# Layer 0's adaLN weight tiles in one list, eleven of them used in the first stage: a two-layer trunk on one Trainium2 core

## The chip, the cores and the metric

The kernel runs on one core of a Trainium2 chip. The metric is the device time of one execution, in microseconds. The engines are called by the names of the profile: PE (TensorE, matrix products; PEld is its weight load), DVE (VectorE), ACT (ScalarE), POOL (GpSimd) and SP (SyncE, which here only issues DMAs, one after the other).

## What is computed

A decoder trunk of two layers on 256 tokens of width 2048, in float32. Layer 0 has a Conformer convolution as its mixer, layer 1 has differential attention, and each layer ends with an MLP of width 8192. Every sub-layer is modulated by six vectors (shift, scale and gate of the mixer, shift, scale and gate of the MLP), which come from one matrix per layer: `cond @ ada_w[i]`, 2048 by 12288, 100 MB in float32 for each layer, read for a single row.

```python
cond = silu(c)
for i in range(2):
    sh_m, sc_m, g_m, sh_f, sc_f, g_f = split(cond @ ada_w[i] + ada_b[i], 6)
    h = x * (1 + sc_m) + sh_m
    y = conformer_conv(h, ...) if i == 0 else diff_attention(h, ...)
    x = layer_norm(ALPHA * x + g_m * y, ...)
    h = x * (1 + sc_f) + sh_f
    y = square(relu(h @ mlp_w1[i] + b1)) @ mlp_w2[i] + b2
    x = layer_norm(ALPHA * x + g_f * y, ...)

def conformer_conv(h, ...):
    a, gt = split(h @ pw1 + b1, 2)              # 2048 -> 4096
    u = a * sigmoid(gt)
    u = causal_depthwise_conv(u, width=31)
    return silu(layer_norm(u, ...)) @ pw2 + b2   # 2048 -> 2048
```

The large products are made to float32 accuracy from three passes: weights and activations are each split in a high part (fp32r, a copy on ACT) and a low part (the rest, a subtraction on DVE), and PE adds up high by high, high by low and low by high.

## The kernel before

**Stages of layer 0, mixer.** pw1 runs in five slices of the contraction dimension (`SLICES`, line 32: 2, 2, 4, 4 and 4 blocks of 128). A slice has 8 output groups of 512 columns and works in *halves*: a half is two blocks by two token tiles by three passes, 12 matmuls. There are 8 halves in each of the first two slices and 16 in each of the others. The slice's partial sums are added up on DVE (`add_up`, line 939). While a slice runs, the adaLN scale and shift for the blocks of the next one are made, in pairs of tiles (`ada_pair`, at the halves in `PAIR_AT`), then finished (`end_ada`, at `END_AT`), and the next slice's h is written (`put_h`, one call for two blocks). The last slice also runs the first convolution steps by a plan (`run_plan`). Behind pw1 comes the *conv tail*, 12 steps (lines 1053 to 1056), then the channel LayerNorm with the *fills* (lines 1065 to 1106), the gate, `swish`, and the product pw2 with its residual (`out_proj`, 16 weight tiles; behind each, `pump_t2` is called once). The MLP of layer 0 follows, then layer 1.

**adaLN tiles.** An adaLN tile is 1024 KB. There are two ways to use one. A *D tile* covers 1024 columns and 2 of the 16 row blocks; DVE multiplies each block by its column of `cond` and adds it up (line 248, two instructions), and after eight tiles PE sums over the partitions (line 231) and DVE adds the bias. A *P tile* covers 512 columns and 4 row blocks; PE multiplies it (line 289), and after four tiles the row is copied by ACT and transposed by PE (line 272). The pairs of the first stage (scale on DVE, shift on PE) are 32 narrower tiles. The 48 *later* tiles are the gate of the mixer and the scale and shift of the MLP: 32 D and 16 P. The gate has to be there before the fills end (line 1086), the others when the MLP begins.

**Two mechanisms.** The pairs are loaded from a list of their own, `ada_load`, five ahead, two more after each pair. The later tiles have a second list, `ada_seq`, of which four are loaded ahead: `ada_ahead` loads one, and `ada_next` uses one and loads another. The first four are loaded in the last slice, at halves 2, 8, 9 and 10; none is used before the conv tail. The tail uses 12 (8 D and 4 P, in the order `ADA_CONV`), the fills use 6 P, and the 16 calls of `pump_t2` spread the other 30 (24 D and 6 P).

**Buffers.** `ada_raw` (line 194) gives each load its home. In the mode "first" five homes take turns: two buffers of their own ("own"), two parts of `ux`, and part of `conv_x`. In the mode "conv" an own buffer alternates with a weight buffer. In the mode "pw2" it is own, part of `ux`, own, part of `conv_x`. `ux` and `conv_x` are the buffers of the convolution and are occupied by it from the middle of the last slice to the end of the tail. A load waits on SP until the tile that had its home before has been used, and later requests on SP stand behind it. pw1's weights are loaded four tiles (eight halves) ahead and split two halves ahead (`split_half`, line 888); a split is a cast on ACT (L481) and a subtraction on DVE (L482).

**Order.** In this first part DVE, ACT and SP run in the order of the program text (`manual_schedule`, line 868), and so does PE throughout. Behind it ACT, SP and POOL are ordered by the framework's planner, DVE again by hand from pw2 on.

Of the kernel before, what the change touches and what calls it, by code (L numbers as in the profile page):

```python
# [19 lines left out]
P = 128  # L20
D = 2048
# [10 lines left out]
SLICES = ((0, 2), (2, 2), (4, 4), (8, 4), (12, 4))  # L32
PAIR_AT = ((1, 3), (0, 2, 3, 5), (1, 4, 7, 10), (1, 4, 7, 10), ())
END_AT = (5, 6, 12, 12, None)
STAGE = ((9, 11), (13, 15), (16, 17), (18, 19), (20, 21), (22, 23), (24, 25), (26, 27))
ADA_CONV = "DPDDPDDPDDPD"
FILL = (1, 1, 2, 2)
ADA_MLP = 66
ADA_WO = 8
ADA_T2 = 16  # L40
# [38 lines left out]
def trunk(  # L79
# [111 lines left out]
    def mod_tile(i, v):  # L191
        return const.tile([P, KC], F32, name=f"mod_{i}_{v}")

    def ada_raw(name):

        homes = {"first": ("own", "own", ux[:, :2048], ux[:, 2048:], conv_x[:, :2048]),
                 "conv": ("own", "weights"), "pw2": ("own", ux[:, 2048:], "own", conv_x[:, :2048])}[n_raw[1]]
        home = homes[n_raw[0] % len(homes)]
        n_raw[0] += 1
        if not isinstance(home, str):  # L200
            return home
        pool, tag = (wraw, "raw") if home == "weights" else (araw, "araw")
        return pool.tile([P, 2048], F32, tag=tag, name=name)

    n_raw = [0, "first"]
    ux = big.tile([P, 4096], F32, tag="uTh", name="conv_ux")
    conv_x = econv.tile([P, 8 * (PAD + S + 1)], F32, name="conv_x")
# [131 lines left out]
                defer(SUM_WAIT, sums)  # L339
        return [lambda kc=kc: step(kc) for kc in range(KC)]  # L340

    ada_q, ahead, later_ada = [], [], {"D": [], "P": []}
# [20 lines left out]
    assert not any(later_ada.values()) and len(ada_seq) == 48  # L363
# [506 lines left out]
    ada_load, ada_step, ada_end = [], [], []  # L870
    for f0, nf in SLICES:
        sc = ada_slice_dve_steps(0, SC_M, f0, nf, m_sc)
        sh = ada_slice_steps(0, SH_M, f0, nf, m_sh, True)
        for a in range(len(sc[0])):
            ada_load.extend([sc[0][a], sh[0][a]])
        ada_step.append([(sc[1][a], sh[1][a]) for a in range(len(sc[0]))])
        ada_end.append((sc[2], sh[2]))
    w_src = [(f"pw1_{g}_{s}", pw1v[:, f0:f0 + nf, :, g * 256:(g + 4 // nf) * 256])
             for s, (f0, nf) in enumerate(SLICES) for g in range(0, NGRP, 4 // nf)]
# [20 lines left out]
    def pending():  # L900
        fns = later[:]
        later.clear()
        for f in fns:
            f()

    def ada_pair(s):
        rows, sh_step = ada_step[s].pop(0)
        n = len(rows) // 2
        for f in rows[:n]:
            f()  # L910
        sh_step()

        def rest():
            for f in rows[n:]:
                f()
            for _ in range(2):
                if ada_load:
                    ada_load.pop(0)()
        later.append(rest)

    def alpha_x(q):

        sl = slice(q * NG, (q + 1) * NG)
        for t in range(NT):
            nc.scalar.activation(z[:, t, sl], z[:, t, sl], AF.Copy, scale=ALPHA)

    def end_ada(s):
        for f in ada_end[s]:
            f()

    def put_h(s, c2):
        f0, nf = SLICES[s]
        if 2 * c2 == f0:
            nc.vector.tensor_scalar(mul[:, f0:f0 + nf], m_sc[:, f0:f0 + nf], 1.0, None, ALU.add)
        to_featT(z, hT, mul, m_sh, "h0", [c2])()
        if c2 % 2:
            later.append(lambda: alpha_x(c2 // 2))
# [5 lines left out]
            else:  # L943
                nc.vector.tensor_tensor(cs[g]["ut"][t], cs[g]["ut"][t], pss[t], op=ALU.add)

    for _ in range(4):
        ada_load.pop(0)()
# [4 lines left out]
    ada_load.pop(0)()  # L952
# [12 lines left out]

# [19 lines left out]

    for j, c in enumerate(STAGE):
        for e in range(2):
            at(c[e] + 1, conv_out, j, e)
    for j, c in enumerate(STAGE):
        for e in range(2):  # L990
            at(c[e] + 2, conv_tok, j, e)
    for j, c in enumerate(STAGE):
        at((4, 6)[j] if j < 2 else STAGE[j - 2][0], glu, j)
    at(23, lambda: nc.scalar.activation(warm, ones[:, 0:1], AF.Silu))
    for j, c in enumerate(STAGE):
        for e in range(2):
            at(c[e], conv_products, j, e)
    for j, c in enumerate(STAGE):
        for b in range(4):
# [14 lines left out]
    for s, (f0, nf) in enumerate(SLICES):  # L1014
        last = f0 + nf == KC
        h = 0
        for g in range(NGRP):
            pss = [mm_bank(f"pw1_{g}_{s}_ps{t}") for t in range(NT)]
            for q in range(nf // 2):
                split_half()  # L1020
                mm_parts(pss, hT, w_parts.pop(0), f0 + 2 * q, f0, f0 + nf - 1)
                pending()
                if h in PAIR_AT[s]:
                    ada_pair(s + 1)
                if not last and h >= END_AT[s]:
# [32 lines left out]
    n_raw[:] = [0, "pw2"]  # L1058

    def fill(n):  # L1060
        for _ in range(n):
# [88 lines left out]
    n_t2 = [0]  # L1150

    def pump_t2():
        n_t2[0] += 1
        if n_t2[0] == 1:
            n_t2.append(len(ahead) + len(ada_seq))
        while len(ahead) + len(ada_seq) > max(0, n_t2[1] * (1 - n_t2[0] / ADA_T2)):
            ada_next()
        if n_t2[0] == GF_LOAD:
            gf_load[0]()
            gf_load[1]()  # L1160
# [313 lines left out]
    for g in range(4):  # L1474
        kv = {}
        pair = lambda: sc1["hT"]
# [85 lines left out]
```

## Time and profile before

| | |
|---|---|
| three runs of before | 2408.17, 2415.34 and 2418.0 us; median 2415.34 |
| the profiled execution | 2417.05 us, of which the span from the first to the last instruction is 2414.5 us |
| mean granted clock of PE | 0.978 |
| busy, share of the span | PE 95%, PEld 75%, DVE 75%, ACT 44%, POOL 10% |
| read from HBM | 604.54 MB; 251 GB/s over the span |

Rows of the profile name an instruction by engine, line, operation, and out<-in by the names of the tiles. In a row of the timeline, the first two numbers are the start and the duration in microseconds, and a bracket at the end gives the idle time of the engine before it and what ended it. In the view by windows each row is a stretch, with its length, the busy time of each engine, PE's granted clock as a share of full speed, the busy share of the 16 DMA engines and the GB/s. In the view of waits, the numbers are microseconds in total, times, and the longest. In a row of the groups, `x` is the count, and after the bar stand busy microseconds, mean nanoseconds of one, and the idle time before. Tiles that are called `aw`, `conv_ux` or `conv_x` and are loaded on line 218 are adaLN tiles; `aacc` is a D tile's sum, `aps` a P tile's.

### The profile page before, as it was taken

Reading aid. Unit: us, or ns where it says so; the run is one execution under the profiler, and the core shown is the slowest. Engines: PE = TensorE matmul, PEld = TensorE weight load, DVE = VectorE, ACT = ScalarE, POOL = GpSimd, SP = SyncE. Lnnn points to the kernel's source line nnn. Section 1 sums busy time; section 2 is a strip of 40 time slices with the busy share of each in tenths; the row PEclk is TensorE's granted clock in tenths of the full one; section 3 lists DMA queues with packets and bytes.
Section 4 is the critical chain, followed back from the end, with each engine's and each line's share of the span. In section 5 each row is a group of like instructions: output and inputs, shape, how many; then the busy total and the mean of one; then the engine's idle time right before and its main releaser. Section 6 shows DMA issues by size and latency. Waiting matters only on the chain.

```text
span 2414.5 us, 28618 instructions
## 1 busy us (share of the span) xinstructions
PE 2287.4 (95%) x11167; PEld 1820.8 (75%) x11167; DVE 1803.1 (75%) x2046; ACT 1057.5 (44%) x1360; POOL 247.9 (10%) x162
## 2 busy tenths in 40 slices
PE   5899988889999999999989999998999999999997
PEld 4577645667778888888877888876788888888886
DVE  5787878879797888877877777886877565565566
ACT  4334753244334434434434445444443443443442
POOL 0000001121330000000024201012213000000002
PEclk9999998989999999999999999998999999999999
DMA  9995389958898888888865666684777555556563
GB/s 347 327 326 199 109 300 367 364 177 321 314 317 313 294 317 289 315 299 307 305 226 181 220 218 227 228 312 164 253 266 225 191 191 192 192 187 194 180 223 104
DMA packets 271980, 608.54 MB, mean 252 GB/s; under 512 B 11038, under 2 KB 44388, under 8 KB 258532
## 3 DMA queue, kind: packets, MB, share of 16 engines
q1 hardware_dynamic: 271604, 606.41, 72.5%
q8 instruction: 87, 1.43, 0.2%
q14 instruction: 49, 0.40, 0.0%
q10 hardware_dynamic: 240, 0.30, 0.0%
HBM read 604.54 MB, written 2.13 MB: 251 GB/s over the span
## 4 chain that ended last, share of the span: by engine, by line
PE 77%; DVE 11%; DMA 5%; issue 3%; ACT 3%; SPq 1%; POOL 1%; DVEq 0%; ACTq 0%; POOLq 0%
PE w_ps L568 18%; PE w_ps L571 18%; PE w_ps L570 18%; DVE aacc L248 2%; DMA aw<-in_ada_w_dram 2%; PE pw_ps L493 2%; PE pw_ps L494 2%; PE pw_ps L495 2%; PE cv L771 2%; DVE wl_w L533 1%; PE qkv_q_ps L571 1%; PE aps L289 1%; PE qkv_q_ps L570 1%; PE qkv_q_ps L568 1%; PE qkv_v_ps L571 1%
## 5 line engine op out<-in xcount | busy, mean ns | idle before, releaser
L533 DVE TENSOR_TENSOR wl_w<-w_w,wh_w 128x1024 fp32r<-128x1024 f32 x502 | 634.4, 1281 | 333.0 <-ACT wh_w L532 332.6
L532 ACT CAST wh_w<-w_w 128x1024 fp32r<-128x1024 f32 x512 | 537.4, 1053 | 763.7 <-PE w_ps L571 589.1
L568 PE MATMUL w_ps<-wh_w,hm_hi 128*128 128x512 f32 x1024 | 403.9, 394 | 4.8 <-ACT hm_hi L401 4.8
L570 PE MATMUL w_ps<-wl_w,hm_hi 128*128 128x512 f32 x1024 | 400.8, 391 | 4.9 <-DVE wl_w L533 4.8
L570 PE MATMUL w_ps<-wl_w,u_hi 128*128 128x512 f32 x1024 | 399.6, 390 | 4.8 <-DVE wl_w L533 4.8
L571 PE MATMUL w_ps<-wh_w,hm_lo 128*128 128x512 f32 x1024 | 401.0, 392 | 0.9 <-DVE hm_lo L404 0.9
L568 PE MATMUL w_ps<-wh_w,u_hi 128*128 128x512 f32 x1024 | 400.5, 391 | 0.0
L571 PE MATMUL w_ps<-wh_w,u_lo 128*128 128x512 f32 x1024 | 399.3, 390 | 0.0
L315 DVE SCALAR_TENSOR_TENSOR acc<-adaw,cond,acc 128x2048 f32<-128x2048 f32 (+1 forms) x105 | 243.1, 2315 | 1.1 <-DMA adaw<-in_ada_w_dram 0.9
L568 PEld LDWEIGHTS w_ps<-wh_w,hm_hi 128*128 128x128 f32 x1024 | 193.5, 189 | 49.1 <-ACT hm_hi L401 6.5
L570 PEld LDWEIGHTS w_ps<-wl_w,hm_hi 128*128 128x128 f32 x1024 | 193.4, 189 | 45.4 <-DVE wl_w L533 6.1
L570 PEld LDWEIGHTS w_ps<-wl_w,u_hi 128*128 128x128 f32 x1024 | 192.5, 188 | 46.2 <-DVE wl_w L533 6.7
L571 PEld LDWEIGHTS w_ps<-wh_w,hm_lo 128*128 128x128 f32 x1024 | 193.3, 189 | 43.1 <-DVE hm_lo L404 2.5
L568 PEld LDWEIGHTS w_ps<-wh_w,u_hi 128*128 128x128 f32 x1024 | 192.6, 188 | 42.4 <-issue 1.7
L571 PEld LDWEIGHTS w_ps<-wh_w,u_lo 128*128 128x128 f32 x1024 | 192.5, 188 | 39.9
L533 POOL TENSOR_TENSOR wl_w<-w_w,wh_w 128x1024 fp32r<-128x1024 f32 x10 | 24.1, 2421 | 1096.7 <-ACT wh_w L532 1096.7
L493 PE MATMUL pw_ps<-wh_pw,h_hi 128*128 128x512 f32 x256 | 106.1, 414 | 12.1 <-ACT h_hi L401 9.3
L482 DVE TENSOR_TENSOR wl_pw<-w_pw,wh_pw 128x1024 fp32r<-128x1024 f32 x64 | 77.7, 1221 | 33.6 <-ACT wh_pw L481 33.3
L494 PE MATMUL pw_ps<-wl_pw,h_hi 128*128 128x512 f32 x256 | 101.8, 398 | 0.5 <-DVE wl_pw L482 0.5
L495 PE MATMUL pw_ps<-wh_pw,h_lo 128*128 128x512 f32 x256 | 101.9, 398 | 0.0
L481 ACT CAST wh_pw<-w_pw 128x1024 fp32r<-128x1024 f32 x64 | 65.9, 1050 | 48.0 <-PE pw_ps L495 40.6
L248 DVE SCALAR_TENSOR_TENSOR aacc<-aw,cond,aacc 128x1024 f32<-128x1024 f32 (+2 forms) x70 | 75.8, 1083 | 2.8 <-DMA aw<-in_ada_w_dram 1.1
(335 smaller groups left out, 3274.7 us busy)
## 6 DMA issues: line engine op xcount, KB each, us to landing
w_w<-in_mlp_w_dram SPq DMA_DIRECT2D x256, 1024.0 KB, 5.2
adaw<-in_ada_w_dram SPq DMA_DIRECT2D x96, 1024.0 KB, 5.2
aw<-in_ada_w_dram SPq DMA_DIRECT2D x48, 1024.0 KB, 10.8
w_pw<-in_conv_pw_w_dram SPq DMA_DIRECT2D x64, 512.0 KB, 9.1
conv_ux<-in_ada_w_dram SPq DMA_DIRECT2D x21, 1024.0 KB, 11.6
w_pw<-in_conv_pw_w_dram SPq DMA_DIRECT2D x16, 1024.0 KB, 10.5
w_qkv_q<-in_attn_qkv_w_dram SPq DMA_DIRECT2D x16, 1024.0 KB, 7.2
w_qkv_k<-in_attn_qkv_w_dram SPq DMA_DIRECT2D x16, 1024.0 KB, 5.0
```

The lines of the kernel that those rows point to most:

```text
L248: nc.vector.scalar_tensor_tensor(st["acc"], wv[:, kc % per, :], cond[:, kc:kc + 1], st["acc"], ALU.mult, ALU.add)
L315: nc.vector.scalar_tensor_tensor(st["acc"], w, cond[:, kc:kc + 1], st["acc"], ALU.mult, ALU.add)
L481: nc.scalar.copy(hq, rq)
L482: nc.vector.tensor_tensor(lq, rq, hq.bitcast(F32), op=ALU.subtract)
L493: nc.tensor.matmul(pss[t], lhsT=xh, rhs=wh, start=(kc == first), stop=False)
L494: nc.tensor.matmul(pss[t], lhsT=xh, rhs=wl, start=False, stop=False)
L495: nc.tensor.matmul(pss[t], lhsT=xl, rhs=wh, start=False, stop=(kc == last))
L532: nc.scalar.copy(hi, rq)
L533: eng.tensor_tensor(lo, rq, hi.bitcast(F32), op=ALU.subtract)
L568: nc.tensor.matmul(pss[tt], lhsT=xh, rhs=wh, start=(kc == 0 and job["bias"] is None), stop=False)
L570: nc.tensor.matmul(pss[tt], lhsT=xh, rhs=wl, start=False, stop=False)
L571: nc.tensor.matmul(pss[tt], lhsT=xl, rhs=wh, start=False, stop=(kc == nk - 1))
```

## The change

All of layer 0's adaLN tiles go into one list, `items`, in the order of use: the pairs of each slice, the new extra tiles between them, the tail's, and those of fills and pw2. Each entry has its mode, its load and its use. `load_ahead` loads while fewer than `limit` are loaded and not used; `used(n)` counts uses and loads on. The limit is 4 at the start, then 5, 2 from half 11 of the fourth slice on, and 4 from half 9 of the last slice on.

Eleven of the later tiles are used in pw1 (`EXTRA`): one D after half 14 of the third slice (blocks 4 to 7), two D after halves 13 and 15 of the fourth, and eight in the last slice: P after halves 0, 4, 8, 10 and 14, D after 2, 6 and 12. The first three have homes of the mode "first"; the eight use a new mode "own", the two own buffers alone. The tail then takes the next 8 D and 4 P, the fills 6 P, and 18 D and 1 P are left for pw2. The mode "pw2" begins with the first fill tile instead of the fifth. Each half of the last slice now ends with a tick, which runs finishes that are due.

At the very start, `end_ada(0)` and `put_h(0, 0)` stand ahead of the first two `split_half()`.

```diff
+EXTRA = ({}, {}, {14: "D"}, {13: "D", 15: "D"},
+         {0: "P", 2: "D", 4: "P", 6: "D", 8: "P", 10: "P", 12: "D", 14: "P"})
-AHEAD_ADA = 4
...
         homes = {"first": ("own", "own", ux[:, :2048], ux[:, 2048:], conv_x[:, :2048]),
-                 "conv": ("own", "weights"), ...
+                 "own": ("own",), "conv": ("own", "weights"), ...
...
-    ada_seq = []
-    for e in ADA_CONV + "P" * sum(FILL) + "DDDDP" * 8:
-        if later_ada[e]:
-            ada_seq.append(later_ada[e].pop(0))
-
-    def ada_ahead():
-        if ada_seq:
-            load, step = ada_seq.pop(0)
-            load()
-            ahead.append(step)
+    def add_items(mode, kinds):
+        for e in kinds:
+            if later_ada[e]:
+                items.append((mode, *later_ada[e].pop(0)))
+
+    def load_ahead():
+        while n_items[1] < len(items) and n_items[1] - n_items[0] < limit[0]:
+            mode, load, _ = items[n_items[1]]
+            if n_raw[1] != mode:
+                n_raw[:] = [0, mode]
+            load()
+            n_items[1] += 1
+
+    def used(n):
+        n_items[0] += n
+        load_ahead()
 
     def ada_next(n=1):
         for _ in range(n):
-            if ahead:
-                ahead.pop(0)()
-                ada_ahead()
+            if n_items[0] < n_items[1]:
+                items[n_items[0]][2]()
+                used(1)
...
+        pair = [[("first", sc[0][a], None), ("first", sh[0][a], None)] for a in range(len(sc[0]))]
+        for h in range(-1, 16):
+            if s == 0 and h < 0:
+                items.extend(i for p in pair for i in p)
+            elif s and h in PAIR_AT[s - 1]:
+                items.extend(pair.pop(0))
+            if s and h in EXTRA[s - 1]:
+                add_items("first", EXTRA[s - 1][h])
+    extra = [EXTRA[-1][h] for h in sorted(EXTRA[-1])]
+    add_items("own", extra)
+    add_items("conv", ADA_CONV)
+    add_items("pw2", "P" * sum(FILL) + "DDDDP" * 8)
...
         def rest():
             for f in rows[n:]:
                 f()
-            for _ in range(2):
-                if ada_load:
-                    ada_load.pop(0)()
+            used(2)
...
+    end_ada(0)
+    put_h(0, 0)
     for _ in range(2):
         split_half()
-    end_ada(0)
-    put_h(0, 0)
...
                 if last:
                     run_plan(h)
-                    if h in (2, 8, 9, 10):
-                        if h == 2:
-                            n_raw[:] = [0, "conv"]
-                        ada_ahead()
+                    tick()
+                    if h == 9:
+                        limit[0] = 4
+                if h in EXTRA[s]:
+                    ada_next()
+                if s == len(SLICES) - 2 and h == 11:
+                    limit[0] = 2
```

More of the change, by code (lines that the diff above doesn't have):

```diff
@@ L194, in ada_raw @@
     def ada_raw(name):
-        homes = {"first": ("own", "own", ux[:, :2048], ux[:, 2048:], conv_x[:, :2048]),
+        homes = {"first": ("own", "own", ux[:, :2048], ux[:, 2048:], conv_x[:, :2048]), "own": ("own",),
                  "conv": ("own", "weights"), "pw2": ("own", ux[:, 2048:], "own", conv_x[:, :2048])}[n_raw[1]]
@@ L340, in ada_steps @@
         return [lambda kc=kc: step(kc) for kc in range(KC)]
-    ada_q, ahead, later_ada = [], [], {"D": [], "P": []}
+    ada_q, items, n_items, limit = [], [], [0, 0], [5]
+    later_ada = {"D": [], "P": []}
     def add_later(eng, v, f0, m):
@@ L358, in trunk @@
     add_later("P", SH_F, 8, m_shf)
-    ada_seq = []
-    for e in ADA_CONV + "P" * sum(FILL) + "DDDDP" * 8:
-        if later_ada[e]:
-            ada_seq.append(later_ada[e].pop(0))
-    assert not any(later_ada.values()) and len(ada_seq) == 48
-    def ada_ahead():
-        if ada_seq:
-            load, step = ada_seq.pop(0)
+    def add_items(mode, kinds):
[7 more added lines that the diff above has]
+                n_raw[:] = [0, mode]
             load()
-            ahead.append(step)
+            n_items[1] += 1
+    def used(n):
+        n_items[0] += n
+        load_ahead()
     def ada_next(n=1):
         for _ in range(n):
-            if ahead:
-                ahead.pop(0)()
-                ada_ahead()
+            if n_items[0] < n_items[1]:
+                items[n_items[0]][2]()
+                used(1)
     m_gf = mod_tile(0, G_F)
@@ L869, in trunk @@
     first_part.__enter__()
-    ada_load, ada_step, ada_end = [], [], []
-    for f0, nf in SLICES:
+    ada_step, ada_end = [], []
+    for s, (f0, nf) in enumerate(SLICES):
         sc = ada_slice_dve_steps(0, SC_M, f0, nf, m_sc)
         sh = ada_slice_steps(0, SH_M, f0, nf, m_sh, True)
-        for a in range(len(sc[0])):
-            ada_load.extend([sc[0][a], sh[0][a]])
         ada_step.append([(sc[1][a], sh[1][a]) for a in range(len(sc[0]))])
         ada_end.append((sc[2], sh[2]))
+        pair = [[("first", sc[0][a], None), ("first", sh[0][a], None)] for a in range(len(sc[0]))]
[10 more added lines that the diff above has]
+    add_items("pw2", "P" * sum(FILL) + "DDDDP" * 8)
+    assert not any(later_ada.values())
     w_src = [(f"pw1_{g}_{s}", pw1v[:, f0:f0 + nf, :, g * 256:(g + 4 // nf) * 256])
@@ L944, in add_up @@
                 nc.vector.tensor_tensor(cs[g]["ut"][t], cs[g]["ut"][t], pss[t], op=ALU.add)
-    for _ in range(4):
-        ada_load.pop(0)()
+    limit[0] = 4
+    load_ahead()
     for t in range(NT):
@@ L951, in trunk @@
         load_w()
-    ada_load.pop(0)()
+    limit[0] = 5
+    load_ahead()
     load_small(0, "conv", [conv_pw1_b[0], conv_dw_b[0], conv_ln_g[0], conv_ln_b[0]])
@@ L1033, in trunk @@
                     run_plan(h)
-                    if h in (2, 8, 9, 10):
-                        if h == 2:
-                            n_raw[:] = [0, "conv"]
-                        ada_ahead()
+                    tick()
+                    if h == 9:
+                        limit[0] = 4
+                if h in EXTRA[s]:
+                    ada_next()
+                if s == len(SLICES) - 2 and h == 11:
+                    limit[0] = 2
                 h += 1
@@ L1057, in trunk @@
     first_part.__exit__(None, None, None)
-    n_raw[:] = [0, "pw2"]
     def fill(n):
@@ L1154, in pump_t2 @@
         if n_t2[0] == 1:
-            n_t2.append(len(ahead) + len(ada_seq))
-        while len(ahead) + len(ada_seq) > max(0, n_t2[1] * (1 - n_t2[0] / ADA_T2)):
+            n_t2.append(len(items) - n_items[0])
+        while len(items) - n_items[0] > max(0, n_t2[1] * (1 - n_t2[0] / ADA_T2)):
             ada_next()
```

## The prediction, on record before the change was run

> **What bounds the kernel now.** I read the page's 40 slices first, to find where the DMA is full and where PE is, and then cut the span into the stages of the code with the view of busy time by windows.
>
> ```profile
> core 0: us, PE busy (x) PEld busy (x) DVE busy (x) ACT busy (x) POOL busy (x), PEclk, DMA share, GB/s
> 32.50:100.00 67.50, 58.71 (x273) 41.69 (x274) 48.42 (x72) 27.11 (x38) 0.00 (x0) 0.93 1.07 372
> ...
> 156.00:207.40 51.40, 51.09 (x246) 38.37 (x246) 42.02 (x56) 20.19 (x24) 0.00 (x0) 1.00 0.71 233
> 207.40:270.80 63.40, 61.26 (x427) 47.17 (x425) 49.01 (x87) 39.18 (x57) 0.00 (x0) 1.00 0.39 134
> 270.80:334.80 64.00, 61.41 (x926) 33.56 (x925) 56.48 (x111) 51.42 (x93) 0.00 (x0) 0.97 0.53 191
> 334.80:355.70 20.90, 12.41 (x85) 5.07 (x84) 9.50 (x23) 12.07 (x20) 0.72 (x1) 0.85 1.04 392
> 355.70:502.30 146.60, 124.06 (x528) 90.48 (x525) 119.58 (x110) 41.61 (x50) 22.69 (x9) 0.88 0.96 358
> 502.30:2414.50 1912.20, 1856.19 (x8388) 1519.85 (x8386) 1421.21 (x1498) 836.14 (x1038) 222.54 (x142) 0.99 0.70 241
> ```
>
> The rows are: early pw1, its fourth slice, its last slice, the conv tail, the fills, pw2, and all the rest. Three readings carry the argument. Up to 100 us the DMA is full (1.07). From 156 to 271 PE is full (51.09 of 51.40 us, 61.26 of 63.40) and the DMA has room (0.71, then 0.39). In the fills and pw2 the DMA is full again (1.04, 0.96), and PE has a low granted clock (0.85, 0.88). After 502 PE is busy 97% of the time with work that the change leaves alone, so a microsecond won or lost before 502 should be one at the end. PE's own waits in pw2, complete:
>
> ```profile
> PE aps L289 <- DMA aw<-in_ada_w_dram: 10.0, 2, 6.0
> PE aps L289 <- DMA conv_x<-in_ada_w_dram: 5.1, 2, 4.8
> PE apt L231 <- DVE aacc L248: 4.6, 2, 3.6
> PE aps L289 <- DMA conv_ux<-in_ada_w_dram: 2.9, 1, 2.9
> ```
>
> 18.0 of 22.6 us are P tiles (the adaLN tiles that PE multiplies, line 289) that stand in PE's queue before their data has landed. None is a wait for pw2's own weights.
>
> **What leaves pw2.** Of the 48 later tiles pw2 takes 30 now (24 for DVE, called D, and 6 P) and 19 afterwards (18 D, 1 P). The tail (8 D, 4 P) and the fills (6 P) keep their counts. One tile is one megabyte:
>
> ```profile
> aw<-in_ada_w_dram SPq DMA_DIRECT2D x48, 1024.0 KB, 10.8
> ```
>
> Eleven are 11.5 MB. At pw2's 358 GB/s that is 32.2 us of DMA, at the 392 of the fills 29.4. PE's side allows as much: five of six P tiles go, and with them up to 18.0 us of waits, 5 x 1.1 us of matmuls (row below) and part of the 146.6 x 0.12 = 17.6 us lost to the clock. DVE's side:
>
> ```profile
> L248 DVE SCALAR_TENSOR_TENSOR aacc<-aw,cond,aacc 128x1024 f32<-128x1024 f32 x21 | 35.1, 1671 | 1.7 <-DMA aw<-in_ada_w_dram 1.1
> ...
> L248 DVE SCALAR_TENSOR_TENSOR aacc<-conv_x,cond,aacc 128x1024 f32<-128x1024 f32 x12 | 17.5, 1458 | 0.3
> L248 DVE SCALAR_TENSOR_TENSOR aacc<-conv_ux,cond,aacc 128x1024 f32<-128x1024 f32 x12 | 17.4, 1451 | 0.3
> ```
>
> These 45 instructions take 70.0 us, 1.56 each; a D tile is two, 3.1 us. The same instruction in the conv tail:
>
> ```profile
> L248 DVE SCALAR_TENSOR_TENSOR aacc<-aw,cond,aacc 128x1024 f32<-128x1024 f32 x15 | 19.2, 1280 | 0.3
> ```
>
> 1.28 us, 2.56 a tile, and POOL is idle there (0.00) where it is busy 22.69 us in pw2. Six D tiles are thus 15.4 to 18.7 us off DVE's 119.6. [...] Nothing in the sum hangs on it: DVE's remaining 101 to 104 us lie under the new length either way.
>
> So the DMA sets the gain. I take -28 us for fills and pw2: a little under 29.4, since at a share of 0.96 not every removed transfer was waited for. Bounds: -15 (only DVE's relief counts) and -38 (the DMA's 32, and some of the clock). What is late next in pw2 is DVE and PE together. For its 384 matmuls PE needs 88 us at the spacing of 0.23 us that full clock gives (rows below), and DVE the 101 to 104 above, both against 146.6 - 28 = 119.
>
> The last four of the six fill tiles change homes: two now wait on SP, in program order, for the conv's last use of its buffers.
>
> ```profile
> L528 SPq DMA_DIRECT2D w_pw<-in_conv_pw_w_dram x3: 464/2202/2415, 331.2 to 339.5; - x3
> ```
>
> ```profile
> L218 SPq DMA_DIRECT2D conv_x<-in_ada_w_dram x1: 2576/2576/2576, 335.2 to 335.2; - x1
> ```
>
> The first request for pw2's weights, at 331.2, may then queue behind a request for conv_x, which before went out at 335.2: at most +4. It also frees two weight buffers that fill tiles held, which may bring it forward by as much. I take 0.
>
> **What the first stage takes on.** P tiles, seen in the fourth slice:
>
> ```profile
> 161.66 0.39 PE L494 MATMUL pw_ps<-wl_pw,h_hi 128*128 128x512 f32 x1
> 161.90 0.39 PE L495 MATMUL pw_ps<-wh_pw,h_lo 128*128 128x512 f32 x1
> 162.21 1.07 PE L289 MATMUL aps<-aw,condr 128*32 128x512 f32 x8
> 163.21 0.50 PE L493 MATMUL pw_ps<-wh_pw,h_hi 128*128 128x512 f32 x1
> ```
>
> From start to start a matmul is 0.23-0.24 us; across the P tile it is 1.31, so the tile costs 1.1. Five in the PE-bound last slice are +5.5, with nothing to hide them; their finishing transposes add 0.5. Six.
>
> D tiles run on DVE in program order, so the weight subtractions (L482) behind them wait 2.56 us. Three lie where DVE is at its latest, at the slice changes, behind the second half's h:
>
> ```profile
> 157.24 0.69 DVE L404 TENSOR_TENSOR h_lo<-h_h,h_hi 128x512 fp32r<-128x512 f32 x1 [1.29 <-ACT h_hi L401]
> 158.19 1.22 DVE L482 TENSOR_TENSOR wl_pw<-w_pw,wh_pw 128x1024 fp32r<-128x1024 f32 x1 [0.26 <-ACT wh_pw L481]
> ```
>
> ```profile
> 159.47 0.50 PE L494 MATMUL pw_ps<-wl_pw,h_hi 128*128 128x512 f32 x1 [0.31 <-DVE wl_pw L482]
> ```
>
> PE already waits 0.31 for this one. The D tile of half 14 falls between the two DVE rows: the subtraction starts 2.56 later less the 0.26 of idle, and PE stops 2.3 us more. At the next change two D tiles come, after halves 13 and 15 (the last rows of this DVE view; its first is used further down):
>
> ```profile
> 195.67 1.22 DVE L482 TENSOR_TENSOR wl_pw<-w_pw,wh_pw 128x1024 fp32r<-128x1024 f32 x1
> ...
> 208.58 0.69 DVE L404 TENSOR_TENSOR h_lo<-h_h,h_hi 128x512 fp32r<-128x512 f32 x1 [1.29 <-ACT h_hi L401]
> 209.53 1.23 DVE L482 TENSOR_TENSOR wl_pw<-w_pw,wh_pw 128x1024 fp32r<-128x1024 f32 x1 [0.26 <-ACT wh_pw L481]
> 210.67 1.28 DVE L944 TENSOR_TENSOR sums<-sums,pw_ps 128x512 f32<-128x512 f32 x2
> 211.87 1.22 DVE L482 TENSOR_TENSOR wl_pw<-w_pw,wh_pw 128x1024 fp32r<-128x1024 f32 x1
> ```
>
> The first moves 209.53 to about 211.9, the second 211.87 to about 217. A half on PE is 12 x 0.23 = 2.8 us, so PE reaches these at about 211.6 (after a P tile) and 215.7 and stops about 1.5 and 2.3 us: +3.8. The three in the last slice meet a DVE that is idle 63.4 - 49.0 = 14.4 us; 7.7 us go into that, but DVE is sometimes late there, so +2. Together +8; bounds 0 (all hidden) and 15.4 (six tiles in full). First stage: 6 + 8 = +14, from +6 to +22.
>
> The SP queue: from the third extra of the last slice on, each tile goes into one of only two buffers, so SP asks for it when the tile two before it has been used, and weight requests stand behind. Landing there, adaLN tiles first, then weights:
>
> ```profile
> DMA to landing us min/median/max: 5.0/6.2/7.4
> ```
>
> ```profile
> DMA to landing us min/median/max: 3.9/4.6/5.2
> ```
>
> Two tiles are four halves apart, 11 us and more. 6.2 fits under that: 0. The tail's first four tiles are asked for at halves 10 to 14 instead of 2 to 10; with 6.2 us to land they are there when the tail begins at 270.8: 0. The tick that each half of the last slice now ends with runs only what the extra tiles have put off (their finishes, counted above). POOL's queue is passed by nothing: it has no work before the fills (0.00 in the rows).
>
> First h ahead of the first casts: the first matmul waited for h_hi behind two casts, and then for DMA.
>
> ```profile
> 32.54 0.79 PE L493 MATMUL pw_ps<-wh_pw,h_hi 128*128 128x512 f32 x1 [7.64 <-ACT h_hi L401]
> ...
> 41.10 1.07 PE L289 MATMUL aps<-aw,condr 128*32 128x256 f32 x16 [1.40 <-DMA aw<-in_ada_w_dram]
> ```
>
> ```profile
> 26.73 1.99 ACT L481 CAST wh_pw<-w_pw 128x1024 fp32r<-128x1024 f32 x2 [5.40 <-DMA w_pw<-in_conv_pw_w_dram]
> ```
>
> The first of these two casts (half of 1.99) and its subtraction (1.22 in the rows above), one after the other from 26.73, let PE begin near 29, 3.5 us sooner. But at 41.10 it waits for a tile of a full DMA, and 1.40 becomes 4.9. I take 0; if that cover is gone, -3.5.
>
> Sum: -28 + 14 = -14. The profiled execution took 2417.05 us, so 2403; the median of before is 1.7 lower, so 2401.
>
> **Rivals.** *More comes back* (0.20). P tiles no longer stop PE in pw2, its clock stays up, and the D tiles hide: -36 + 8 = -28, so 2415.3 - 28 = 2387. For it: the P waits and the clock of 0.88. Against it: the L494 wait at 159.47.
>
> *DVE takes over pw2* (0.15). DVE is busy 119.58 of 146.6 us, in one order, with casts between tiles. If that order paces pw2, only the 15.4 us of six tiles come off, against +14: 2415.3 - 1.4 = 2414, no change. Against: PE's waits for DVE there are only 4.6.
>
> *SP holds the weights back* (0.10), the way to slower. The third tile for the two buffers is asked for when the last pair of adaLN tiles has been used, just before the DVE row at 195.67, and SP then stands until the last slice's first P tile has run: 207.4 + 2.8 + 1.1, near 211. The next weights behind are wanted ten halves after 196, 27.6 us; 12 are left. Tile ahead (2.7 us of transfer), landing, cast and subtraction (2.3) must fit, so it decides from a landing of 7 us. At 11, PE stops 4 us here and at each of five later requests: +24 on the +14, less 28, is +10: 2425. Against: 4.6 and 6.2. [...]
>
> **How the numbers follow.** Forecast 0.55, its own range 2391 to 2412 (half the spread of each term). A measurement of this kernel can tell 0.5%, 12 us: below 2403.3 is faster. Forecast gives 0.33 faster and 0.22 the same; with the first rival, faster 0.53; with the second, the same 0.37; slower 0.10. The range, 2384 to 2419, takes in the first rival to a little past its middle and the second with some of its spread; outside lie the third (0.10) and the far end of the first.
>
> **What would show it.** Right: the first matmul near 29 and the next wait for a tile at 41 unmoved; pw1 ends some 14 us later than 270.8, with L494 waits at both slice changes; the tail is as long as before (64.0); fills and pw2 are 28 us shorter than 20.9 + 146.6, with hardly a P wait and a clock above 0.88. Wrong: PE waiting for ACT casts that wait for w_pw in the last slice (third rival); pw2 still 130 us or more with DVE over 95% busy (second); the first stage no longer at all (first).

## The result, and the profile after

| | before | after |
|---|---|---|
| median of the runs, us | 2416.33 (2408.17 to 2418.0, 4 runs) | 2393.42 (2391.37 to 2394.6, 4 runs) |
| the profiled execution, and its span, us | 2417.05, 2414.5 | 2392.5, 2390.7 |
| mean granted clock of PE | 0.978 | 0.987 |

The ratio is 0.9911, with a 95% interval from 0.9887 to 0.9935: 23 us by the medians, where 14 were forecast, and inside the range. The view by windows of the kernel after, cut at the same places as that of before in the prediction (early pw1, its last slice, the tail, the fills, pw2, and everything from the MLP's first product on), with the last stretch of before behind it:

```profile
32.50:100.00 67.50, 56.64 (x280) 40.00 (x278) 46.37 (x72) 25.26 (x36) 0.00 (x0) 0.95 1.05 368
...
209.00:283.30 74.30, 69.47 (x472) 49.28 (x472) 58.89 (x98) 39.93 (x58) 0.00 (x0) 1.00 0.57 192
283.30:353.30 70.00, 65.17 (x944) 36.31 (x943) 59.28 (x117) 55.48 (x97) 0.00 (x0) 0.98 0.60 218
353.30:372.60 19.30, 10.31 (x69) 4.10 (x68) 7.22 (x18) 8.60 (x17) 0.72 (x1) 0.82 1.05 393
372.60:484.30 111.70, 105.97 (x484) 82.57 (x480) 106.83 (x96) 39.93 (x47) 22.98 (x9) 0.98 0.97 358
...
491.00:2390.70 1899.70, 1848.03 (x8355) 1515.08 (x8355) 1413.08 (x1484) 833.38 (x1029) 217.09 (x140) 0.99 0.71 242
```

```profile
514.20:2414.50 1900.30, 1850.78 (x8359) 1517.31 (x8355) 1409.51 (x1481) 830.91 (x1028) 214.77 (x137) 0.99 0.70 242
```

The last slice and the tail are longer, fills and pw2 much shorter (131.0 us for 167.5), and in pw2 PE now runs at 0.98 of its clock where it ran at 0.88. The DMA is as full there as before (0.97, 358 GB/s). PE's own waits in the fills, and then in pw2, complete:

```profile
PE aps L290 <- DMA conv_x<-in_ada_w_dram: 7.0, 1, 7.0
PE aps L290 <- DMA conv_ux<-in_ada_w_dram: 1.6, 1, 1.6
PE aps L290 <- DMA aw<-in_ada_w_dram: 0.4, 1, 0.4
```

```profile
PE pw_ps L580 <- DVE wl_pw L543: 5.6, 2, 4.4
```

In pw2 there is no P wait left, and the one kind of wait is for DVE.

For the stages below I use four landmarks of each trace: the last pw1 matmul, the end of the last convolution matmul (the tail's end), the end of the last pw2 matmul, and the first matmul of the MLP. Before they are at 270.4, 334.1, 502.5 and 514.2, after at 282.7, 353.0, 484.3 and 490.9. So pw1 gives 12.4 us away and the tail 6.6; fills and pw2 win 37.1; the change from pw2 to the MLP wins 5.1 (11.7 to 6.7); the rest wins 0.5. That makes the 23.8 between the two spans.

Differences of 2 to 3 us near 110 us, behind the stretch where the DMA is full (1.06 from 100 to 104 us, before), are taken as no evidence: in the trace of before and in the four below whose program is the same up to there, one and the same subtraction of DVE lies between 106.4 and 108.6 us.

### The profile page after: what moved, and what is told of

It reads as the page before. It is cut to its first block, busy times and chain, and to the rows that moved or that the text cites. A ratio compares the mean times of both kernels' runs of the same rounds, so it can differ in the third digit from the quotient of the medians.

```text
span 2390.7 us, 28609 instructions
## 1 busy us (share of the span) xinstructions
PE 2276.4 (95%) x11167; PEld 1814.2 (76%) x11167; DVE 1802.4 (75%) x2046; ACT 1059.9 (44%) x1360; POOL 247.6 (10%) x162
## 4 chain that ended last, share of the span: by engine, by line
PE 78%; DVE 12%; DMA 4%; issue 3%; ACT 2%; POOL 1%; SPq 1%; DVEq 0%; ACTq 0%; POOLq 0%
PE w_ps L578 18%; PE w_ps L581 18%; PE w_ps L580 18%; DVE aacc L249 2%; PE cv L781 2%; PE pw_ps L503 2%; PE pw_ps L504 2%; PE pw_ps L505 2%; DVE wl_w L543 1%; DVE acc L316 1%; PE qkv_q_ps L581 1%; PE qkv_q_ps L580 1%; PE qkv_q_ps L578 1%; PE qkv_v_ps L581 1%; PE qkv_v_ps L578 1%
## 5 line engine op out<-in xcount | busy, mean ns | idle before, releaser
L503 PEld LDWEIGHTS pw_ps<-wh_pw,h_hi 128*128 128x128 f32 x256 | 49.3, 192 | 40.1 <-issue 15.6
```

The lines of the kernel that those rows point to most:

```text
L503: nc.tensor.matmul(pss[t], lhsT=xh, rhs=wh, start=(kc == first), stop=False)
```

## The experiments

Medians of each kernel, each against the kernel before on the same chip, and the landmarks of its trace (fills and pw2: from the tail's end to the last pw2 matmul):

| kernel | median, us | ratio to before, 95% interval | tail's end | fills and pw2 |
|---|---|---|---|---|
| before | | | 334.1 | 168.4 |
| after | 2393.42 | 0.9911 [0.9887, 0.9935] | 353.0 | 131.3 |
| before, eleven loads shared | 2407.92 | 0.9976 [0.9965, 0.9987] | 333.1 | 158.3 |
| before, eleven uses cut | 2405.33 | 0.9969 [0.9959, 0.9979] | 334.2 | 154.7 |
| before, both | 2391.53 | 0.9910 [0.9896, 0.9925] | 333.0 | 145.7 |
| before, both, finishes later | 2386.48 | 0.9889 [0.9876, 0.9903] | 332.0 | 138.9 |
| after, homes of before | 2398.05 | 0.9941 [0.9922, 0.9959] | 352.8 | 134.3 |
| after, casts first | 2395.65 | 0.9930 [0.9909, 0.9950] | 352.6 | 131.6 |
| after, P tiles only | 2400.75 | 0.9941 [0.9921, 0.9960] | 336.0 | 149.2 |
| after, D tiles only | 2415.04 | 1.0008 [0.9997, 1.0020] | 357.4 | 145.1 |
| after, D tiles in mid-slice | 2394.97 | 0.9925 [0.9912, 0.9939] | 348.6 | 133.5 |
| after, early pw2 weights | 2404.16 | 0.9965 [0.9952, 0.9977] | 360.9 | 133.3 |
| after, eight tiles | 2400.89 | 0.9944 [0.9930, 0.9958] | 341.2 | 147.4 |

There is one trace of each kernel, so a difference of 2 or 3 us between two stages rests on single executions: the work from the MLP's first product to the end, the same in all, takes 1898.7 to 1902.8 us in these traces. The four runs of "P tiles only" span 2393.9 to 2402.8 us, and its trace is that of the lowest. The trace of "before, both" is that of its highest run (2395.32 us; the other three lie between 2390.6 and 2391.7).

**The bytes alone.** The kernel before, with eleven loads left out and the tile ahead used twice.

```diff
         def load(a):
+            if share[0]:
+                return share[1].rearrange("p (j n) -> p j n", n=w)
-            t = ada_raw(f"aw_{i}_{v}_{f0}_{a}")
+            t = share[1] = ada_raw(f"aw_{i}_{v}_{f0}_{a}")
...
+    shared = [k for k in range(18, 47) if (k - 18) % 5 in (1, 4)][:11]
```

> The kernel before, with eleven of pw2's thirty adaLN loads left out: six D tiles and five P tiles are computed from the tile that the D tile ahead of them has loaded, so that every instruction of DVE and PE stays and only 11.5 MB of transfers go (the modulation vectors come from partly wrong weights). If the bytes set the length of fills and pw2 (my theory), their 167.5 us fall by 11.5 MB at 358 to 392 GB/s, 29 to 32 us, and the run by about 30, to about 2386. If DVE paces pw2 (the second rival), nothing goes: 0 to -5 us.

Pw2 in the view by windows, and PE's waits from the fills to the MLP that are for DVE:

```profile
354.10:491.37 137.27, 124.74 (x530) 92.67 (x527) 120.60 (x110) 41.48 (x50) 23.18 (x9) 0.88 0.81 299
```

```profile
PE apt L234 <- DVE aacc L251: 11.1, 3, 5.9
...
PE pw_ps L583 <- DVE wl_pw L546: 1.4, 2, 0.9
```

The DMA is no longer full (0.81), and yet fills and pw2 win 10.1 us and not 29 to 32. The P waits of pw2 are gone with the loads (18.0 us before, none here), but PE stops 11.1 us for D sums that DVE hasn't made, and its clock is as low as before (0.88). The sum of the prediction, bytes over GB/s, falls here.

**The uses alone.** All loads stay; six D tiles are not multiplied, and five P tiles multiply resident data.

```diff
-                nc.tensor.matmul(st["ps"][r:r + 32, :], lhsT=condr[:, kc, :], rhs=wv[:, kc % per, :],
+                nc.tensor.matmul(st["ps"][r:r + 32, :], lhsT=condr[:, kc, :],
+                                 rhs=condr.rearrange("p k c -> p (k c)") if cut[0] else wv[:, kc % per, :],
...
+    def cut_step(k, tv, step):
+        nc.gpsimd.tensor_copy(junk, tv[:, 0, 0:1])
+        if (k - 18) % 5 == 4:
+            cut[0] = True
+            step()
+            cut[0] = False
```

> The kernel before, with all of its loads, but the same eleven tiles are hardly used: the six D tiles are not multiplied (twelve DVE instructions of 1.56 us go, 18.7 us), the five P tiles multiply data that is resident, so that PE doesn't wait for their landing, and one GpSimd instruction on one column touches each of the eleven tiles (the modulation vectors are not computed rightly). If the bytes set the length of fills and pw2, next to nothing goes: 0 to -6 us, and the P waits come back as waits for pw2's own weights. If DVE paces pw2: -15. If the stops of PE behind P tiles and the clock that falls in them are the cost themselves (the first rival's mechanism): -15 to -30.

One of its ten executions, the profiled one, took 11139 us, with matmuls of the MLP at 1.4 us each, for a cause that its trace doesn't show. The other nine lie between 2402.1 and 2407.4, and the median in the table is theirs; the stages come from an eleventh execution, of 2406.79 us.

> The experiment with all loads and eleven uses cut, once more, for its profile. New theory: DMA is full through fills and pw2 (0.95 or more of the time), DVE has 18 us less to do than before there, and the stretch is 5 to 9 us shorter. Rival (the stops behind P tiles are the cost): DMA falls to 0.9 and PE's clock rises above 0.95.

Pw2:

```profile
355.37:488.84 133.47, 120.63 (x530) 89.29 (x527) 103.00 (x98) 41.48 (x50) 30.23 (x19) 0.92 1.03 394
```

The run won 7.4 us by the medians (2412.74 and 2405.33), fills and pw2 13.7 in the trace, more than the 0 to 6 and then 5 to 9 that I gave it. The signs of the rival, a DMA share of 0.9 and a clock above 0.95, did not come (1.03, 0.92). The DMA now runs without a hole: 133.47 us at 394 GB/s are 52.6 MB, what pw2 moved before in 146.6 us at 358 (52.5 MB). Here the bytes do bound it, 13 us below the old length.

**Both.** The eleven tiles are neither loaded nor used in pw2.

```diff
+        while ada_seq:
             load, step = ada_seq.pop(0)
...
+            if k not in cuts:
+                load()
+                ahead.append(step)
+                break
+            ahead.append(lambda k=k, step=step: cut_step(k, step))
...
```

> The kernel before, with the eleven tiles of the two experiments above neither loaded nor used in pw2 (their part of the modulation vectors is missing; of the five P tiles' matmuls only two tiles' worth stay, on resident data, to open and close the sums). Leaving out the loads alone brought 5 us, leaving out the uses alone 7. If DMA and DVE are two bounds of nearly the same length, so that each alone is held by the other (my new theory), both together bring far more than 12: 30 to 37 us, fills and pw2 130 to 137 us long, the run near 2378. If the effects add (rival): 12 us, 2400.

Fills and pw2 win 22.7 us, the run 22.8 by the medians. Both expectations miss. In fills and pw2 the two effects nearly add (10.1 + 13.7 = 23.8); by the medians of the runs they don't (4.8 + 7.4 = 12.2 for 22.8), so whether they add stays open. And 14.4 us of what the real change wins in fills and pw2 are still lacking. Its pw2, the wait there, PE at that place, and four stretches of 1 us around it:

```profile
354.24:478.71 124.47, 117.45 (x506) 90.49 (x503) 105.86 (x98) 41.23 (x50) 21.52 (x9) 0.90 0.90 330
```

```profile
PE apt L232 <- DVE aacc L249: 7.0, 2, 4.6
```

```profile
421.52 0.39 PE L591 MATMUL pw_ps<-wh_pw,swish_lo 128*128 128x512 f32 x1
426.51 3.58 PE L232 MATMUL apt<-ones,aacc 128*128 128x1 f32 x16 [4.60 <-DVE aacc L249]
```

```profile
423.00:424.00 1.00, 0.00 (x0) 0.00 (x0) 0.96 (x2) 0.04 (x1) 0.00 (x0) 0.95 0.65 250
428.00:429.00 1.00, 1.00 (x6) 1.00 (x6) 0.96 (x2) 0.00 (x0) 0.00 (x0) 0.50 0.96 348
433.00:434.00 1.00, 1.00 (x4) 0.72 (x3) 0.00 (x0) 0.00 (x0) 0.00 (x0) 0.50 1.05 408
434.00:435.00 1.00, 1.00 (x6) 0.82 (x5) 0.00 (x0) 0.06 (x1) 0.00 (x0) 0.93 1.05 428
```

A D sum's finish (L232) stands in PE's order and waits 4.60 us; the clock is at 0.50 at 428 and at 433, and back only at 434. One stop is paid twice. It is the same behind a P wait: in the kernel before, PE's stop of 6.02 us that ends at 370.63 is followed by a granted clock of 0.50 until 376.9.

**Finishes later.** The same, with two finishes three half-jobs further back.

```diff
             if kc == KC - 1:
-                defer(DVE_WAIT, finish)
+                defer(DVE_WAIT + 3 * (v == SC_F), finish)
```

> The experiment that leaves out loads and uses of eleven tiles, with the finishes of the two D sums that end within pw2 put off by three more half-jobs of PE. There fills and pw2 took 145.7 us and not the 131.3 of the changed kernel, although the same tiles are gone; PE stood 7.0 us for DVE's sums (4.6 and 2.4), and its clock was 0.58 to 0.60 for some 12 us behind the first. If such a stop costs itself and the clock behind it (my theory): both stops go, 7 us and some 5 to 6 us of clock, pw2 from 124.5 to 111 to 115, the run near 2380. If PE only waits there for a DVE that is the bound anyway: the wait comes back as a wait for pw2's own low parts, and pw2 stays within 3 us of 124.5.

Pw2, and its waits:

```profile
353.13:470.90 117.77, 113.53 (x506) 87.02 (x503) 105.57 (x98) 41.24 (x50) 20.84 (x9) 0.94 0.95 348
```

```profile
PE pw_ps L590 <- DVE wl_pw L553: 2.8, 1, 2.8
PE apt L232 <- DVE aacc L249: 1.4, 1, 1.4
```

124.5 us become 117.8, a little short of the 111 to 115. Of 7.0 us of stops 1.4 stay and 2.8 come back as a wait for DVE, and the clock rises from 0.90 to 0.94. The stops cost 6.7 us by the traces, without a byte or a DVE instruction less. By the ratios of the runs (0.9910 and 0.9889) it is 5 us.

**Homes of before.** The first four fill tiles of the changed kernel in the mode "conv".

```diff
-    add_items("pw2", "P" * sum(FILL) + "DDDDP" * 8)
+    add_items("conv", "PPPP")
+    add_items("pw2", "PP" + "DDDDP" * 8)
```

> The changed kernel, with the homes of the first four fill tiles as before (own buffer and weight buffer in turn). In the changed kernel four of pw2's weight tiles are requested before the tail ends, in the kernel before two. If it is the freed weight buffers that bring these forward (I took 0 for it), then the tail moves about 2 MB less here (218 GB/s falls toward 190), fills and pw2 are 4 to 6 us longer than the 131.0 of the changed kernel, and the run goes to about 2398. If the homes do nothing: within 1 us of 131.0.

The tail:

```profile
282.50:352.81 70.31, 66.21 (x943) 36.82 (x942) 58.66 (x116) 51.22 (x92) 0.00 (x0) 0.95 0.52 194
```

194 GB/s for the changed kernel's 218, and fills and pw2 3.0 us longer. The mechanism is as expected and the size a little smaller: the new homes leave the weight buffers to pw2's weights, and 1.7 MB more come in the tail (70.23 us at 219 GB/s, for 70.31 at 194).

**Casts first.** Only the order at the start is undone.

```diff
+    for _ in range(2):
+        split_half()
     end_ada(0)
     put_h(0, 0)
-    for _ in range(2):
-        split_half()
```

> The changed kernel, with the first two weight splits ahead of the first h again. My theory: the first matmul goes back from 27.9 to about 32.5 us, the DMA wait at 41.2 shrinks from 4.7 to about 1.4 us, and from there on nothing differs: 0. If the early start is worth something by itself (a tile used sooner frees its buffer sooner): +3.5 us at 100 us and at the end.

The first matmul is at 32.51, and the MLP begins at 490.86 for 490.92. By the traces the early first h is worth nothing; the intervals of the two kernels in the table overlap.

**P tiles only, D tiles only.** The eleven tiles divided. In the first, loads of the mode "own" are asked for only while fewer than two tiles are out.

```diff
-EXTRA = ({}, {}, {14: "D"}, {13: "D", 15: "D"},
-         {0: "P", 2: "D", 4: "P", 6: "D", 8: "P", 10: "P", 12: "D", 14: "P"})
+EXTRA = ({}, {}, {}, {},
+         {0: "P", 4: "P", 8: "P", 10: "P", 14: "P"})
```

```diff
+EXTRA = ({}, {}, {14: "D"}, {13: "D", 15: "D"},
+         {2: "D", 6: "D", 12: "D"})
```

> The changed kernel, with only the five P tiles taken up in the last slice (24 D and 1 P are left for pw2). By the prediction's terms the last slice pays 6 us. New theory: DVE keeps all its 24 D tiles and holds pw2 at about the 137 us that it had with the loads alone left out, so fills and pw2 take 155 to 160 us: -8 to -12 there, -3 to -6 for the run, near 2409. If every tile that leaves is worth the same (rival, 36.5 us by 5 of 11): fills and pw2 151, the run -10.

> The changed kernel, with only the six D tiles taken up in the first stage (18 D and 6 P are left for pw2). By the prediction's terms the first stage pays 8 us (+2.3 at the slice change at 157, +3.8 at the next, +2 in the last slice). New theory: DVE is relieved and the DMA decides: 6.3 MB and the 1.6 MB that the homes bring forward at 358 to 392 GB/s, 20 to 22 us less in fills and pw2 than 167.5, and the run 12 to 16 us below before. If every tile that leaves is worth the same (rival, 36.5 us by 6 of 11): much the same, -20; this one shows the cost in the first stage above all.

The five P tiles win 19.2 us in fills and pw2 and give 2.0 away by the tail's end; DVE with all its D tiles doesn't hold pw2 at 137 (128.9 in the trace), so that expectation falls, and the rival's 151 for fills and pw2 is close to the 149.2. PE's waits in its pw2, and that stretch:

```profile
PE pw_ps L581 <- DVE wl_pw L544: 13.4, 7, 5.3
PE aps L290 <- DMA aw<-in_ada_w_dram: 0.3, 1, 0.3
```

```profile
356.28:485.20 128.92, 115.23 (x484) 87.38 (x480) 120.85 (x108) 40.00 (x47) 23.73 (x9) 0.92 0.96 359
```

The P waits are gone, PE waits for DVE instead, which is busy 94% of the stretch, and the clock is 0.92 and not 0.98. The six D tiles win 23.3 and lose 23.3, so that the 12 to 16 us expected of that run don't come. Of the loss 17.3 us are in pw1, where 8 were expected. ACT's and PE's waits there, and the adaLN requests on SP:

```profile
ACT wh_pw L491 <- DMA w_pw<-in_conv_pw_w_dram: 15.5, 1, 15.5
```

```profile
PE pa L812 <- DVE vtok L963: 9.8, 3, 8.8
```

```profile
L219 SPq DMA_DIRECT2D aw<-in_ada_w_dram x2: 368/1204/2041, 197.6 to 225.8; - x2
```

From 197.6 to 225.8 SP stands at a load for a buffer that is free only when the D tile ahead of it has run, pw1's weights wait behind, ACT stands 15.5 us before its next cast, and PE stops 8.8 us. That is the third rival, at its place. With the P tiles between them, in the changed kernel, SP stands from 196.6 to 213.4, and no cast waits for a weight:

```profile
L219 SPq DMA_DIRECT2D aw<-in_ada_w_dram x2: 368/860/1353, 196.6 to 213.4; - x2
```

**Three attempts at a better kernel.** D tiles in mid-slice (first diff), pw2's weights in the tail (second), and eight tiles (third). The first and the third keep the rule on loads of the kernel with P tiles only.

```diff
+EXTRA = ({}, {}, {}, {2: "D", 5: "D", 8: "D"},
+         {0: "P", 2: "D", 4: "P", 6: "D", 8: "P", 10: "P", 12: "D", 14: "P"})
```

```diff
-    add_items("conv", ADA_CONV)
+    add_items("own", ADA_CONV)
...
-                    if h == 9:
-                        limit[0] = 4
...
+        if n < 4:
+            t = wraw.tile([P, 2048], F32, tag="raw", name=f"w_pw2_0_{n}")
+            pre[f"pw2_0_{n}"] = (t, nc.sync.dma_start(t.rearrange("p (a n) -> p a n", a=4),
+                                                      pw2v[:, 4 * n:4 * n + 4, 0:NG]))
+        if n == 9:
+            limit[0] = 4
```

```diff
+EXTRA = ({}, {}, {}, {2: "D", 5: "D", 8: "D"},
+         {0: "P", 4: "P", 8: "P", 10: "P", 14: "P"})
```

> The changed kernel, with the three D tiles that stand at the slice changes moved into the fourth slice, after halves 2, 5 and 8 (and the loads of the last slice's extra tiles asked for only while fewer than two are out). By DVE's own clock, the splits of the halves behind the three tiles came 1.6, 2.2 and 2.5 us later than in the kernel with P tiles only. In the fourth slice DVE is busy 42 of 51 us, so there they should hide: the first stage 4 to 6 us shorter than the changed kernel's, fills and pw2 as they are (131 us), the run near 2389. If DVE's order has no room there either: within 2 us of the changed kernel.

> The changed kernel, with pw2's first four weight tiles asked for at the first four steps of the tail, where the DMA moved 219 GB/s, and the tail's own adaLN tiles in the two own buffers alone. If the bytes in the full stretch are what counts: two more megabytes leave it, so fills and pw2 are 4 to 6 us shorter than 131.3, as long as the tail's tiles still land in time (5.5 us of landing against two steps of 5.4 us each). If PE and DVE are the bound of pw2 by now (PE was busy 106.0 of 111.7 us there), only the 7.0 us wait in the fills can shrink: 0 to -4 us. If two buffers are too few for the tail: the tail grows by 2 to 6 us, and the run is slower.

> The changed kernel with eight extra tiles in place of eleven: the five P tiles of the last slice, and three D tiles in the fourth slice, after halves 2, 5 and 8; the three D tiles of the last slice go back to pw2 (21 D and 1 P there). With the P tiles alone the tail ended at 336.0 and pw2 at 485.2 us; the three D tiles in the fourth slice put DVE's splits back by 2.4 us. If three bounds of about the same length hold fills and pw2 (bytes, DVE's order, and PE with its stops), the three D tiles take about 9 us from the 149.2: tail's end 338 to 339, pw2's end 478 to 480, and the run some 5 us under the changed kernel, 2386 to 2389. If the eleven tiles are needed, pw2 ends at 483 or later and the run is no faster than the changed kernel's 2393.

In mid-slice the D tiles hide as expected: pw1 ends at 278.8 for 282.7, and the tail 4.4 us earlier. Fills and pw2 take 2.2 us more and the step to the MLP 1.0, and the time can't be told from the changed kernel's. With two buffers the tail grows from 70.2 to 78.1 us, as its last rival said, and fills and pw2 win nothing (133.3 us; by their rates 47.5 MB in that trace, for 47.7). With eight tiles the guess was wrong: pw2 took 126.0 us, with two stops of the kind above,

```profile
PE apt L232 <- DVE aacc L249: 5.9, 1, 5.9
PE pw_ps L581 <- DVE wl_pw L544: 5.2, 3, 2.8
PE aps L290 <- DMA aw<-in_ada_w_dram: 4.4, 1, 4.4
```

a D sum's finish that falls into pw2 again, and its last P tile. None of the three beats the changed kernel.

## Why the prediction was right, and where it was not

**Fills and pw2, -28.** Measured -36.5 by the same cuts, at the far end of the bounds, and the step "the DMA sets the gain" failed. Eleven tiles less are 11.5 MB, but the bytes alone won 10.1 us: after that the DMA is no longer full (0.81 in pw2), and PE waits for DVE. DVE, which was to be busy 101 to 104 us of 119, is busy 106.8 of 111.7 in the changed kernel. By the traces the 37.1 us are about: 10 from the bytes and 14 from the uses (together 22.7), 7 from stops of PE at finishes and the clock behind them, and 3 from the homes. That leaves some 5 open. Adding these up is itself an assumption: the stops were taken out of the kernel before, the homes out of the changed one. The same division by kinds of tile, 19.2 for P (in its fastest run) and 23.3 for D, adds up to 42.5, of which the homes are counted twice. The account of bytes looks perfect, and misleads: fills and pw2 move 13.1 MB less (60.7 to 47.6), which at 358 GB/s is 36.6 us. Several bounds lay close together here (pw2 took 137.3 us with the bytes gone and 133.5 with the uses gone), and a length fits each of them.

**"I take 0" for the homes.** It was the second half of that sentence, the freed weight buffers: -3.

**First stage, +14.** pw1 ends 12.4 later. Ahead of the first extra tile, at 151, the changed kernel was 2.4 us early, a difference of the kind that is no evidence, so the extra tiles cost 14.8. With P tiles only, pw1 ends 1.7 us late after being 2.6 early at 155: 4.3 us for the P tiles. In the last slice they add 6.0 us to PE's busy time (60.9 to 66.8), the 6 that were said; but PE had been idle for 2.1 us there, and some of them went into that, which "nothing to hide them" had left out. The D tiles make the rest, for which 8 were said: pw1 ends 10.7 us later with them than without. The wait for the D tile of half 14 came where it was put:

```profile
158.68 0.50 PE L504 MATMUL pw_ps<-wl_pw,h_hi 128*128 128x512 f32 x1 [1.95 <-DVE wl_pw L492]
```

**Tail, 0.** It took 6.6 us more. Six D tiles have gone ahead, so that a D sum ends within the tail and is finished there. The finish costs PE 1.95 us, and the next D sum uses the same buffer, so DVE's first instruction of it waits 4.98 us until PE has read the old sum:

```profile
310.79 1.95 PE L232 MATMUL apt<-ones,aacc 128*128 128x1 f32 x16
```

```profile
312.78 0.75 DVE L247 TENSOR_SCALAR aacc<-aw,cond 128x1024 f32<-128x1024 f32 x1 [4.98 <-PE apt L232]
```

DVE works in one order, and behind this PE waits for the convolution's copies and for ACT (4.7 us in the tail, 2.6 before). The finish belongs to the D tiles: the tail takes 64.0 us with P tiles only and 69.7 with D tiles only. The prediction counted the tail's tiles, which are the same, and not its finishes. No run moved this finish by itself, so how the 6.6 us divide is not shown.

**First h, 0.** Right, and for its reason:

```profile
27.94 0.80 PE L503 MATMUL pw_ps<-wh_pw,h_hi 128*128 128x512 f32 x1 [2.93 <-ACT wh_pw L491]
```

```profile
41.22 1.08 PE L290 MATMUL aps<-aw,condr 128*32 128x256 f32 x8 [4.72 <-DMA aw<-in_ada_w_dram]
```

The first matmul was to be near 29, the wait at 41 to stay and to be 4.9.

**After pw2.** "A microsecond won or lost before 502 should be one at the end" missed 5.1 us; they are in the last section.

**The rivals.** The first gave -36 for fills and pw2 by P waits and clock, and its number came: the P waits of pw2 are gone and the clock is 0.98. The median, 2393.42, lies about midway between the forecast's 2401 and this rival's 2387. But the P waits alone are not the cause: they are gone as well with the loads left out, and but for 0.3 us with P tiles only, where all D tiles are still used in pw2, and there the clock is 0.88 and 0.92, and PE waits for DVE (12.5 and 13.4 us in pw2). The second is a part of the truth: with the bytes gone, PE waits for DVE. Its 15.4 us are six tiles at the tail's 1.28 us an instruction; in pw2, with the uses gone, DVE is busy 103.0 us for 119.6, 16.6 less for the same twelve instructions. The third is real, as the D tiles alone show, and does no harm here, since the tile whose buffer SP waits for is used at half 0 and not at half 2.

Errors of both signs (-8.5 in fills and pw2, -5.1 behind them, +6.6 in the tail) partly hid one another. That the time came out closer than the steps was in part luck.

One phrase of the second rival needs setting right: the casts between DVE's tiles in pw2 are subtractions (line 533, 27.6 us for pw2's weights), and POOL does seven more of them there (20.8 us).

## What to carry to other kernels

Where a stretch is full on several engines, take one load off at a time before saying which bounds it: here the bytes alone gave 10 us, the work alone 14, both 23, and only with fewer stops of PE and the new homes on top did the stretch lose 37. Work in an in-order queue that waits for another engine, a finish above all, belongs where its data is surely there (in "before, both" a finish stood 4.60 us in PE's queue, and the granted clock was 0.50 for 7.5 us behind it); moved work takes its finishes along (the tail took 69.7 us with D tiles only and 64.0 with P tiles only). A request for a buffer that comes free late may go on a shared queue only if nothing urgent stands behind it (with D tiles only SP stood from 197.6 to 225.8, and ACT 15.5 us before a cast).

## What the hardware showed

**The clock behind a stop.** The 4.60 us stop above (before, both) was followed by a granted clock of 0.50 until 434, 7.5 us after PE had begun again; the first 3.6 of these were sixteen one-column matmuls. The clock fell at 423.9, 2.0 us after PE had stopped. In the same kernel a second stop, of 2.42 us between 460.04 and 466.26, was followed by a mean clock of 0.57 in the next 6.23 us. In pw2 of the kernel before it fell 2.1 us (stop to 370.63) to 3.9 us (to 458.91) after PE had stopped. The way back took, in the same pw2, 3.4 us (stop to 458.91) to 6.3 (to 370.63) behind stops that ended in ordinary matmuls, and 8.7 behind the one that ended in one-column matmuls (to 487.69). Whether the one-column matmuls make it longer is not shown: no run tried it by itself.

**Tiny DVE instructions beside a POOL subtraction.** Before, between pw2 and the MLP, DVE and then POOL:

```profile
503.71 2.31 DVE L727 TENSOR_SCALAR hm_s<-mod 128x16 f32<-128x16 f32 x1
506.05 2.26 DVE L728 SCALAR_TENSOR_TENSOR hm_mul<-cols_ln,hm_s 128x16 f32<-128x16 f32 x1
```

```profile
500.96 7.32 POOL L533 TENSOR_TENSOR wl_w<-w_w,wh_w 128x1024 fp32r<-128x1024 f32 x3 [0.98 <-ACT wh_w L532]
```

After, the same DVE instruction, and POOL's next subtractions behind it:

```profile
484.49 0.17 DVE L737 TENSOR_SCALAR hm_s<-mod 128x16 f32<-128x16 f32 x1
```

```profile
486.16 4.87 POOL L543 TENSOR_TENSOR wl_w<-w_w,wh_w 128x1024 fp32r<-128x1024 f32 x2 [2.60 <-ACT wh_w L542]
```

Sixteen columns took 2.31 and 2.26 us while POOL subtractions of 2.44 on average ran, and 0.17 where none did; the MLP's first h waits for this chain (ACT 4.5 us for `hm_add`, before). What held the two instructions up, no run shows. PE's stop for this h is 4.0 us shorter after (6.49 to 2.46), which is most of the 5.1 us won there, but no run moved POOL's subtractions by themselves.
